# Hybrid encoder block on one core: q in two DRAM tensors, v in SBUF, and an earlier first latent head

## The chip, the core and the metric

One core of a Trainium2 chip runs the whole kernel. The metric is the device time of one execution in microseconds, the median of several runs. The engines are TensorE (PE, with its weight loads as PEld), VectorE (DVE), ScalarE (ACT), GpSimd (POOL) and SyncE (SP), which here only issues DMA transfers. All loads and stores go through SP's one queue, in its order, to 16 DMA engines.

## What is computed

One layer of a bidirectional encoder, 1024 tokens by 1024 features: a SwiGLU block, a mixer, a second SwiGLU block, each between RMS norms and added to the residual. The mixer has one input projection whose columns feed a latent attention (8 heads), a dilated windowed attention (8 heads) and two gates. The part that matters here is the latent attention:

```
q      = (rms_norm(cq) @ w_uq).reshape(S, 8, 64 + 32)      # 64 plain, 32 rotary columns a head
k_nope = (rms_norm(ckv) @ w_uk).reshape(S, 8, 64)
v_a    = (rms_norm(ckv) @ w_uv).reshape(S, 8, 64)
k_a    = concat([k_nope, rope(kr) for every head])
o_a    = softmax(q k_a^T * 96**-0.5) @ v_a                 # dense, 1024 x 1024 a head
```

All products are made to near-float32 accuracy: each operand is split into a high and a low part (`split`, L520: ACT copies the rounded high part, POOL subtracts it), and a product takes three matmuls (`three`, L285).

## The kernel before, in words

**Order of the work.** The stages are Python generators that a planner (`Plan`, L126 to L211) steps through at build time. Each generator yields an engine with a cost (`pe`, `act`, `dve`, `pool`, `dma`, L262 to L278), an `Event` or a `Tokens` count, and the planner serves each engine's queue by rank. The moment at which it calls a step sets where that step is written in the program. The framework's scheduler then fixes the order on each engine; it may put a step ahead of one that was written earlier and whose input or buffer is not there yet. On the chip each engine works strictly in that order.

**Buffers.** SBUF tiles come from three rings: `slot` (21 of 4 KB a partition), `half_slot` (7 of 2 KB) and `big` (14 of 8 KB), L237 to L244. A tile waits until one of its ring is free. In PSUM there are four single banks (`B1`) and two pairs of banks (`S2`).

**Before the stage.** After the first SwiGLU block, the normed input is held, transposed and split, in 8 `big` tiles (`Xm`) until the last column group of the input projection has used it. The column groups ("fillers", `filler_weights` and `chunk_projection`, L1310 and L1421) fill PE while other stages wait. Groups 0 to 3 run before the latent projections, groups 4 to 13 from then on (`HELD`, L113; `m2_done`, L1515).

**The latent projections** (`latent`, from L1656). The compressed q and kv (`cth`, `ctl`: four `big` tiles and two slots) are multiplied by the split weights. For each half of the tokens: `q_rope` (the rotary columns, turned by POOL, transposed, stored), `q_rows(0)`, `k_rows(0)`, four `v_tile`. Then, for head pairs 1 to 3, `q_rows` and `k_rows` of both halves. Each product ends in one PSUM bank; `keep_rows` (L1701) copies it on ACT into a half slot and stores it on SP. Pair i's q of one half is 128 rows by 512 columns in SBUF; in DRAM `qT_d` has 96 rows a head, so the store's target is 2 blocks of 64 rows:

```
rows = qT_d[192 * i : 192 * i + 192, halves[hf]].rearrange("(h e) c -> h e c", e=96)
spawn(keep_rows(ps, qscale, [(rows[:, 0:64, :], 0, P)], [pair_ready[i]]), 4)
```

and the rotary rows of four heads go to 4 blocks of 32 rows (L1753). The rows of k (`kT_d`, L1772) are 128 whole rows that lie together. v goes to `va_d`, 128 whole rows a tile (L1780).

**The heads** (`mla`, L1957; `mla_prep`, L1829). For a head, `mla_prep` loads q (96 rows), then k (64 rows) and the shared rotary k (32 rows), and splits each into two `qkT` slots (ACT, then DVE for q and POOL for k), then loads this head's 64 columns of v from `va_d` (256-byte pieces) and splits them into `vv`. One `nat_tok` lets one of the two loads be prepared at a time. `mla` starts head 0 when `v_written` is set, takes two `proj_tok`, and then starts `mla_prep(0)`; head h+1 is prepared during the second pair of head h. `mla_tile` (L1869) makes one tile of 128 queries: six score matmuls, row maximum on DVE, exponential on ACT (L1892), scaling on POOL (L1902), transposes on PE with casts into a `pt` tile (a `big`; four tokens). `mla_pair` multiplies by `vv`.

Of the kernel before, what the change touches and what calls it, by code (L numbers as in the profile page):

```python
# [9 lines left out]
F32 = mybir.dt.float32  # L10
F32R = mybir.dt.float32r
# [5 lines left out]
S = 1024  # L17
D = 1024
DFF = 2816
P = 128  # L20
NT = S // P
# [104 lines left out]
class Plan:  # L126
# [17 lines left out]
    def spawn(self, gen, rank=5):  # L144
        self.alive.add(gen)
        self._at(self.now, lambda: self._step(gen, rank))
# [73 lines left out]
def _build(tc, es, a, consts, out, dbg):  # L220
# [3 lines left out]
    dr = es.enter_context(tc.tile_pool(name="dr", bufs=1, space=bass.MemoryType.DRAM))  # L224
    V, A, G, T = nc.vector, nc.scalar, nc.gpsimd, nc.tensor
    load = nc.sync.dma_start
    plan = Plan()
    spawn = plan.spawn
# [8 lines left out]
    def slot(shape, dt=F32, name="u"):  # L237
        return sb.tile(shape, dt, tag="u", bufs=NU, name=nm(name))

    def half_slot(shape, dt=F32, name="t"):  # L240
        return sb.tile(shape, dt, tag="t", bufs=NH, name=nm(name))

    def big(shape, dt=F32R, name="g"):
        return sb.tile(shape, dt, tag="g", bufs=NG, name=nm(name))  # L244
# [14 lines left out]
    B1 = Tokens(4)  # L259
# [5 lines left out]
    def act(n, fn):  # L265
        return ("act", 0.04 + n * 0.00088, fn)
# [10 lines left out]
    def dma(kb, fn):  # L277
        return ("dma", kb / 350.0, fn)  # L278
# [19 lines left out]
    kr = keep([P, NT, 32], F32, "kr")  # L298
# [221 lines left out]
    def split(src, hi, lo, n):  # L520
        yield act(n, lambda: A.copy(hi, src))  # L521
        yield pool(n, lambda: G.tensor_sub(lo, src, hi))  # L522
# [609 lines left out]

    h1 = dr.tile([S, D], F32, name="h1")
    h2 = dr.tile([S, D], F32, name="h2")
    qT_d = dr.tile([768, S], F32, name="qT_d")
    kT_d = dr.tile([512, S], F32, name="kT_d")
    kr_d = dr.tile([32, S], F32, name="kr_d")
    va_d = dr.tile([S, 512], F32, name="va_d")
    dqT_d = dr.tile([512, S], F32, name="dqT_d")
    dkT_d = dr.tile([512, S], F32, name="dkT_d")  # L1140
    dv_d = dr.tile([S, 512], F32, name="dv_d")
    lg_d = dr.tile([2 * D, S], F32, name="lg_d")
    ya_d = dr.tile([D, S], F32, name="ya_d")
    oa_d = dr.tile([512, S], F32, name="oa_d")
    ob_d = dr.tile([512, S], F32, name="ob_d")
# [393 lines left out]
    kr_ready, m2_done = Event(NT), Event()  # L1539
    pair_ready, rope_ready, v_ready = [Event(4) for _ in range(4)], Event(6), Event(NT)  # L1540
    v_written = Event()

    def latent():
        yield ffn1_done
# [113 lines left out]
        for c in range(3):  # L1658
            bx = []
# [41 lines left out]
        def keep_rows(ps, scale, stores, evs):  # L1701

            bx = []

            def cp():
                o = half_slot([P, 512], name="o")
                A.mul(o, ps, scale)
                bx.append(o)

            yield act(512, cp)  # L1710
            plan.release(B1)

            def st_():
                for dst, r0, r1 in stores:
                    load(dst, bx[0][r0:r1, :])

            yield dma(256, st_)
            for e in evs:
                plan.set(e)

        def q_rope(hf):

            qr = slot([P, 4, 256], name="qr")
            ready = Event(4)

            def turned(j, ps):
                yield act(256, lambda: A.mul(qr[:, j, :], ps[:, :256], qscale))
                plan.release(B1)
                yield rot_ready
                yield from rope(qr[:, j, :].rearrange("p (h two f) -> p h two f", h=8, two=2), 4 * hf + j, 0, 16)  # L1730
                plan.set(ready)

            for j in range(4):
                ts = slice((4 * hf + j) * P, (4 * hf + j + 1) * P)
                ps = yield from product(256, [
                    (cth[c][:, ts], ctl[c][:, ts], wuq[c][0][:, 512:768], wuq[c][1][:, 512:768]) for c in range(3)
                ])
                spawn(turned(j, ps), 3)

            def rest():  # L1740
                yield ready
                for i in range(2):
                    yield B1
                    bb = []

                    def tr():
                        b = bank()
                        for j in range(4):
                            T.transpose(b[:, j * P : (j + 1) * P], qr[:, j, P * i : P * i + P], ident)
                        bb.append(b)  # L1750

                    yield pe(1024, tr)
                    rows = qT_d[384 * i : 384 * i + 384, halves[hf]].rearrange("(h e) c -> h e c", e=96)  # L1753
                    yield from keep_rows(bb[0], 1.0, [(rows[:, 64:96, :], 0, P)], [rope_ready])

            spawn(rest(), 3)

        def q_rows(i, hf):
            ps = yield from product(512, [
                (wuq[c][0][:, P * i : P * i + P], wuq[c][1][:, P * i : P * i + P], cth[c][:, halves[hf]], ctl[c][:, halves[hf]])  # L1760
                for c in range(3)
            ])
            rows = qT_d[192 * i : 192 * i + 192, halves[hf]].rearrange("(h e) c -> h e c", e=96)
            spawn(keep_rows(ps, qscale, [(rows[:, 0:64, :], 0, P)], [pair_ready[i]]), 4)

        def k_rows(i, hf):
            wh, wl = wkv[0]
# [6 lines left out]
        def v_tile(t):  # L1774
            ts = slice(t * P, (t + 1) * P)
            wh, wl = wkv[1]
            ps = yield from product(512, [
                (cth[3 + c][:, ts], ctl[3 + c][:, ts], wh[:, c, :], wl[:, c, :]) for c in range(2)
            ])
            spawn(keep_rows(ps, 1.0, [(va_d[ts, :], 0, P)], [v_ready]), 3)  # L1780

        def k_rope():
            yield kr_ready
# [45 lines left out]
    def mla_prep(h, hb, ev):  # L1829
        yield pair_ready[h // 2]  # L1830
        yield rope_ready
        for which in range(2):
            yield nat_tok
            bx = Box()

            def ld():
                bx.n = slot([96, S], name="nat")
                if which == 0:
                    load(bx.n, qT_d[96 * h : 96 * h + 96, :])
                else:  # L1840
                    load(bx.n[0:64, :], kT_d[64 * h : 64 * h + 64, :])
                    load(bx.n[64:96, :], kr_d)

            yield dma(512, ld)
            tt = [slot([P, S], F32R, "qkT") for _ in range(2)]
            if which == 0:
                hb.qT = tt
            else:
                hb.kT = tt
            yield act(S, lambda: A.copy(tt[0][:96, :], bx.n))  # L1850
            yield QKSUB[which](S, lambda: (V if QKSUB[which] is dve else G).tensor_sub(tt[1][:96, :], bx.n, tt[0][:96, :]))
            plan.release(nat_tok)

        yield v_ready

        def ldv():
            hb.vn = half_slot([P, NT, 64], name="vn")
            load(hb.vn, va_d[:, 64 * h : 64 * h + 64].rearrange("(t p) c -> p t c", p=P))

        yield dma(400, ldv)  # L1860
        hb.vv = slot([P, NT, P], F32R, "vv")
        yield from split(hb.vn, hb.vv[:, :, 0:64], hb.vv[:, :, 64:128], 512)
        plan.set(ev)

    p_tok = Tokens(3)
# [90 lines left out]

    def mla():  # L1957
        yield v_written
        yield proj_tok
        yield proj_tok  # L1960
        ready = [Event() for _ in range(8)]
        hbs = [Box() for _ in range(8)]
        spawn(mla_prep(0, hbs[0], ready[0]), 3)
        for h in range(8):
            yield ready[h]
            hb = hbs[h]
            hev = Event(4)
            if h == GATES_FROM:
                plan.set(gates_on)
            if h == 7:  # L1970
                plan.set(mla_half)
            for pr in range(4):
                pb = Box()
                pev = [Event(2), Event(2)]
                pb.pt, pb.got = [None, None], [Event(), Event()]

                for qi in range(2):
                    yield p_tok
                    spawn(mla_tile(h, hb, 2 * pr + qi, pb, pev), 2)
                spawn(mla_pair(h, hb, pr, pb, pev, hev), 2)  # L1980
                if pr == 1 and h < 7:
                    spawn(mla_prep(h + 1, hbs[h + 1], ready[h + 1]), 2)

            def fin(ev):
                yield ev
                plan.set(oa_done)
                if oa_done.left == 0:
                    plan.release(pd_tok)

            spawn(fin(hev), 2)  # L1990
# [577 lines left out]
    spawn(second(), 6)  # L2568
    plan.run()
    if dbg is not None:  # L2570
        for nme, src in dict(h1=h1, h2=h2, qT=qT_d, kT=kT_d, kr=kr_d, va=va_d, dqT=dqT_d, dkT=dkT_d, dv=dv_d, lg=lg_d, oa=oa_d, ob=ob_d).items():
            if nme in dbg:
                load(dbg[nme], src)

# [28 lines left out]
```

## Time and profile before

| what | value |
|---|---|
| time, median of 3 runs | 2509.57 us (2507.45 to 2510.3) |
| the profiled execution: its own time | 2505.2 us |
| the profiled execution: span of its instructions | 2503.2 us |
| PE busy | 2311.5 us, 92% of the span |
| mean granted TensorE clock | 0.964 |

The span runs from the first to the last instruction; the 2.0 us between it and the execution's own time lie around it. A line such as "L1850 ACT CAST qkT<-nat [9.72 <-DMA nat<-kr_d]" is read as: the cast of line 1850, which writes qkT from nat, started after its engine had been idle for 9.72 us, and what ended the idle time was the landing of the load of nat from kr_d. SP has no busy time; its rows show how long an issue took. The granted clock has two levels, 1.00 for 2.4 GHz and 0.50 for 1.2 GHz; means lie between.

### The profile page before, as it was taken

The page shows a single profiled execution, that of the slowest core. Times are in us where ns is not written, and L with a number is a line of the kernel's source. Part 1 is how long each engine was busy: PE and PEld are TensorE (multiplying, and loading weights), DVE is VectorE, ACT ScalarE, POOL GpSimd, SP SyncE. Part 2 cuts the span into 40 slices and gives each one's busy share as a digit, 9 for nine tenths or more (in the row PEclk, how much of TensorE's full clock was granted, in tenths as well). Part 3 has the DMA queues.
Part 4 walks back from the last instruction along what each step waited for, and adds up shares of the span by engine and source line. Part 5 has one row for each costly group of instructions (what it writes and reads, how often), then busy time and mean ns, then how long its engine had stood idle before and what let it go on. Part 6 is the DMA issues. An engine that isn't in the chain of part 4 may idle for free. (4 is left out here: it accounts for less than half of the span.)

```text
span 2503.2 us, 30709 instructions
## 1 busy us (share of the span) xinstructions
PE 2311.5 (92%) x11096; PEld 1930.7 (77%) x11096; DVE 1595.3 (64%) x2667; ACT 1042.4 (42%) x1958; POOL 797.8 (32%) x592
## 2 busy tenths in 40 slices
PE   6999999989979995999998889998879999999996
PEld 4888888778769984888887777776668888877885
DVE  8887777655582103666667676347877778773757
ACT  6343343321153334656655555454343334343211
POOL 2000000354483534656543232576300000023545
PEclk8999999999989997999999999899989999999998
DMA  4253443777251233122222222575434434457762
GB/s 152 101 181 126 156 164 130 268 294 259 103 191 45 70 111 96 51 60 73 81 73 84 81 83 70 180 249 197 147 101 168 160 133 170 150 186 286 275 221 101
DMA packets 198007, 364.84 MB, mean 146 GB/s; under 512 B 40608, under 2 KB 112800, under 8 KB 197344
## 3 DMA queue, kind: packets, MB, share of 16 engines
q1 hardware_dynamic: 197856, 362.89, 42.6%
q8 instruction: 87, 1.43, 0.2%
q14 instruction: 64, 0.52, 0.1%
HBM read 240.02 MB, written 122.81 MB: 145 GB/s over the span
## 5 line engine op out<-in xcount | busy, mean ns | idle before, releaser
L675 PE MATMUL s<-xh,wt 128*128 128x512 f32 x1408 | 452.9, 393 | 13.2 <-DVE uu L771 12.2
L522 POOL TENSOR_TENSOR wdb<-rawd,wdb 128x1024 fp32r<-128x1024 f32 x34 | 87.4, 2574 | 958.7 <-ACT wdb L521 958.7
L675 PE MATMUL b<-xh,wt 128*128 128x512 f32 x1056 | 343.4, 392 | 1.9 <-ACT uu L744 0.7
L675 PEld LDWEIGHTS s<-xh,wt 128*128 128x128 f32 x1408 | 266.3, 189 | 72.4 <-issue 13.3
L675 PE MATMUL s<-xl,wt 128*128 128x512 f32 x704 | 275.7, 392 | 0.0
L675 PEld LDWEIGHTS b<-xh,wt 128*128 128x128 f32 x1056 | 199.2, 189 | 44.5 <-DVE wt L649 1.1
L675 PE MATMUL b<-xl,wt 128*128 128x512 f32 x528 | 206.5, 391 | 0.6 <-DVE xl L431 0.6
L1079 PE MATMUL b<-wdb,ha 128*128 128x512 f32 x864 | 203.1, 390 | 3.4 <-POOL wdb L522 3.4
L1079 PE MATMUL s<-wdb,ha 128*128 128x512 f32 x816 | 195.4, 395 | 9.0 <-DVE bacc L1028 4.4
L1079 PEld LDWEIGHTS b<-wdb,ha 128*128 128x128 f32 x864 | 162.3, 188 | 38.0 <-POOL wdb L522 4.3
L1079 PEld LDWEIGHTS s<-wdb,ha 128*128 128x128 f32 x816 | 155.1, 190 | 44.0 <-DVE bacc L1028 5.2
L1442 PE MATMUL b<-xh,wh 128*128 128x512 f32 x384 | 163.4, 425 | 0.0
L1902 POOL TENSOR_TENSOR p<-p,rd 128x1024 f32<-128x1024 f32 x64 | 121.8, 1910 | 104.0 <-DVE rd L1899 102.8
L649 DVE TENSOR_TENSOR wt<-s,wt 128x512 fp32r<-128x512 f32 x176 | 120.1, 710 | 54.1 <-ACT wt L648 54.1
L675 PEld LDWEIGHTS s<-xl,wt 128*128 128x128 f32 x704 | 133.3, 189 | 26.9
L1442 PE MATMUL b<-xl,wh 128*128 128x512 f32 x384 | 153.7, 400 | 0.0
L1442 PE MATMUL b<-xh,wl 128*128 128x512 f32 x384 | 153.6, 400 | 0.0
L522 POOL TENSOR_TENSOR wdb<-td,wdb 128x1024 fp32r<-128x1024 f32 x40 | 107.6, 2694 | 71.4 <-ACT wdb L521 71.4
L426 PE MATMUL b<-cst,p 128*128 128x128 f32 x768 | 107.9, 282 | 23.8 <-DVE ptd L431 14.7
L522 POOL TENSOR_TENSOR wl<-raw,wh 128x512 fp32r<-128x512 f32 (+3 forms) x88 | 108.4, 1250 | 48.7 <-ACT wh L521 42.0
L283 PE MATMUL s<-qkT,qkT 96*128 96x512 f32 x384 | 103.2, 404 | 21.5 <-ACT p L1892 21.5
L426 PEld LDWEIGHTS b<-cst,p 128*128 128x128 f32 x768 | 91.5, 145 | 40.9 <-DVE ptd L431 17.3
(290 smaller groups left out, 5003.2 us busy)
## 6 DMA issues: line engine op xcount, KB each, us to landing
hs_d<-hl SPq DMA_DIRECT2D x140, 512.0 KB
ha<-hs_d SPq DMA_DIRECT2D x70, 1024.0 KB
raw<-in_ffn_w_gate_dram SPq DMA_DIRECT2D x44, 512.0 KB
raw<-in_ffn_w_up_dram SPq DMA_DIRECT2D x44, 512.0 KB
rawd<-in_ffn_w_down_dram SPq DMA_DIRECT2D x44, 512.0 KB
raw<-in_w_in_dram SPq DMA_DIRECT2D x28, 512.0 KB
h<-res SPq DMA_DIRECT2D x16, 512.0 KB
lg_d<-lg SPq DMA_DIRECT2D x32, 256.0 KB
```

The costliest lines, as they stand in the source:

```text
L283: T.matmul(o, l, r, start=(i == 0), stop=(i == n - 1))
L426: T.transpose(b[:rows, i * P : (i + 1) * P], src(i), ident)
L522: yield pool(n, lambda: G.tensor_sub(lo, src, hi))
L649: yield dve(512, lambda: V.tensor_sub(w[:, 1], src, w[:, 0]))
L675: T.matmul(out(), l, r, start=(first and k == 0 and n == 0), stop=(k == 3 and n == 2), skip_group_check=True,)
L1079: T.matmul(ps, l, r, start=(fresh and n == 0), stop=(n == 5), skip_group_check=True)
L1442: T.matmul(bs.ps, l, r, start=(part == 0 and n == 0), stop=(part == 7 and n == 2))
L1902: yield pool(S, lambda: G.tensor_tensor(bx.p, bx.p, bx.rd.broadcast_to([P, S]), op=ALU.mult))
```

## The change

q is kept in DRAM as two tensors, `qn_d` with the 64 plain rows of every head and `qr_d` with the 32 rotary rows, so that each store writes 128 whole rows that lie together; a head's load of q becomes two loads. v is kept in two `big` tiles of SBUF (`va`), from which each head's `vv` is split in two halves; the store to and the loads from `va_d` are gone. Head 0's split q takes a `big` tile in place of two slots, and `mla` starts `mla_prep(0)` before it takes the two `proj_tok`.

```diff
-    qT_d = dr.tile([768, S], F32, name="qT_d")
+    qn_d = dr.tile([512, S], F32, name="qn_d")
+    qr_d = dr.tile([256, S], F32, name="qr_d")
...
-    va_d = dr.tile([S, 512], F32, name="va_d")
...
+    va = [None, None]
...
-                    rows = qT_d[384 * i : 384 * i + 384, halves[hf]].rearrange("(h e) c -> h e c", e=96)
-                    yield from keep_rows(bb[0], 1.0, [(rows[:, 64:96, :], 0, P)], [rope_ready])
+                    yield from keep_rows(bb[0], 1.0, [(qr_d[P * i : P * i + P, halves[hf]], 0, P)], [rope_ready])
...
-            rows = qT_d[192 * i : 192 * i + 192, halves[hf]].rearrange("(h e) c -> h e c", e=96)
-            spawn(keep_rows(ps, qscale, [(rows[:, 0:64, :], 0, P)], [pair_ready[i]]), 4)
+            spawn(keep_rows(ps, qscale, [(qn_d[P * i : P * i + P, halves[hf]], 0, P)], [pair_ready[i]]), 4)
...
-            spawn(keep_rows(ps, 1.0, [(va_d[ts, :], 0, P)], [v_ready]), 3)
+            spawn(keep_v(ps, t), 3)
+
+        def keep_v(ps, t):
+            def cp():
+                if t % 4 == 0:
+                    va[t // 4] = big([P, 4, 512], F32, name="va")
+                A.copy(va[t // 4][:, t % 4, :], ps)
+
+            yield act(512, cp)
+            plan.release(B1)
+            plan.set(v_ready)
...
-                    load(bx.n, qT_d[96 * h : 96 * h + 96, :])
+                    load(bx.n[0:64, :], qn_d[64 * h : 64 * h + 64, :])
+                    load(bx.n[64:96, :], qr_d[32 * h : 32 * h + 32, :])
...
-            tt = [slot([P, S], F32R, "qkT") for _ in range(2)]
+            if h == 0 and which == 0:
+                hl = big([P, 2, S], name="qk0")
+                tt = [hl[:, 0, :], hl[:, 1, :]]
+            else:
+                tt = [slot([P, S], F32R, "qkT") for _ in range(2)]
...
-        def ldv():
-            hb.vn = half_slot([P, NT, 64], name="vn")
-            load(hb.vn, va_d[:, 64 * h : 64 * h + 64].rearrange("(t p) c -> p t c", p=P))
-
-        yield dma(400, ldv)
         hb.vv = slot([P, NT, P], F32R, "vv")
-        yield from split(hb.vn, hb.vv[:, :, 0:64], hb.vv[:, :, 64:128], 512)
+        for kb in range(2):
+            ks = slice(4 * kb, 4 * kb + 4)
+            yield from split(va[kb][:, :, 64 * h : 64 * h + 64], hb.vv[:, ks, 0:64], hb.vv[:, ks, 64:128], 256)
...
         yield v_written
-        yield proj_tok
-        yield proj_tok
         ready = [Event() for _ in range(8)]
         hbs = [Box() for _ in range(8)]
         spawn(mla_prep(0, hbs[0], ready[0]), 3)
+        yield proj_tok
+        yield proj_tok
```

## Rows read from the trace of the kernel before

**Rows 1.** The page, part 1: busy time, share of the span, instructions.

```profile
PE 2311.5 (92%) x11096; PEld 1930.7 (77%) x11096; DVE 1595.3 (64%) x2667; ACT 1042.4 (42%) x1958; POOL 797.8 (32%) x592
```

**Rows 2.** Stretches: length, busy of PE PEld DVE ACT POOL, clock, DMA share, GB/s.

```profile
935.00:945.00 10.00, 2.92 (x13) 2.11 (x13) 0.00 (x0) 1.79 (x3) 0.67 (x1) 0.90 0.21 78
...
955.00:965.00 10.00, 0.00 (x0) 0.00 (x0) 0.00 (x0) 0.00 (x0) 0.00 (x0) 0.50 0.28 90
965.00:975.00 10.00, 1.94 (x5) 1.55 (x6) 0.33 (x2) 5.60 (x12) 4.48 (x5) 0.50 0.52 149
```

**Rows 3.** Waits of PE, 860 to 1000: total us, times, longest.

```profile
PE s L283 <- ACT p L1892: 21.5, 1, 21.5
PE b L283 <- ACT o L1707: 8.6, 2, 7.1
```

**Rows 4.** Waits of ACT, 880 to 985: total us, times, longest.

```profile
ACT o L1707 <- DMA qT_d<-o: 6.7, 3, 2.9
```

**Rows 5.** Timeline of SP's queue: start, time of the issue, transfer.

```profile
932.69 1.16 SPq L1842 DMA_DIRECT2D nat<-kr_d  x1
...
934.92 4.90 SPq L1715 DMA_DIRECT2D kT_d<-o  x1
...
955.17 4.77 SPq L1858 DMA_DIRECT2D vn<-va_d  x1
```

**Rows 6.** Single microseconds as stretches; the last two columns are the DMA's.

```profile
937.00:938.00 1.00, 0.72 (x4) 0.26 (x2) 0.00 (x0) 0.00 (x0) 0.00 (x0) 1.00 0.13 49
940.00:941.00 1.00, 0.00 (x0) 0.00 (x0) 0.00 (x0) 0.00 (x0) 0.00 (x0) 1.00 0.69 260
...
964.00:965.00 1.00, 0.00 (x0) 0.00 (x0) 0.00 (x0) 0.00 (x0) 0.00 (x0) 0.50 0.13 49
```

**Rows 7.** Timeline of PE: start, length, line, form, count, idle before.

```profile
928.54 0.74 PE L283 MATMUL b<-ct,wuh 128*128 128x512 f32 x2 [1.54 <-ACT o L1707]
...
937.33 0.39 PE L283 MATMUL b<-cth,wul 128*128 128x512 f32 x1
944.80 1.22 PE L283 MATMUL b<-ct,wuh 128*128 128x512 f32 x2 [7.08 <-ACT o L1707]
...
947.52 4.01 PE L283 MATMUL s<-qkT,qkT 96*128 96x512 f32 x12
973.06 2.93 PE L283 MATMUL s<-qkT,qkT 96*128 96x512 f32 x6 [21.52 <-ACT p L1892]
...
983.95 0.48 PE L1442 MATMUL b<-xh,wh 128*128 128x512 f32 x1
```

**Rows 8.** Timeline of ACT: the casts of head 0 and the first exponential.

```profile
926.95 1.04 ACT L1850 CAST qkT<-nat 96x1024 fp32r<-96x1024 f32 x1 [6.08 <-DMA nat<-qT_d]
...
943.21 1.04 ACT L1850 CAST qkT<-nat 96x1024 fp32r<-96x1024 f32 x1 [9.72 <-DMA nat<-kr_d]
...
969.17 0.62 ACT L521 CAST vv<-vn 128x512 fp32r<-128x512 f32 x1 [20.27 <-DMA vn<-va_d]
...
970.51 1.28 ACT L1892 ACT_TABLE_LOAD   x1
971.80 1.11 ACT L1892 ACTIVATE p<-s,negm 128x1024 f32<-128x1024 f32 x1
```

**Rows 9.** Timeline of DVE: head 0's first row maximum.

```profile
950.18 1.23 DVE L1886 TENSOR_REDUCE negm<-s 128x1 f32<-128x1024 f32 x1 [20.93 <-PE s L283]
```

**Rows 10.** The tile qkT: q's subtraction, ns min/median/max, first and last start.

```profile
L1851 DVE TENSOR_TENSOR qkT<-nat,qkT x8: 1202/2024/3316, 928.0 to 1218.1; 96x1024 fp32r<-96x1024 f32 x8
```

**Rows 11.** The tile vn: v's subtraction on POOL, ns min/median/max.

```profile
L522 POOL TENSOR_TENSOR vv<-vn,vv x8: 1262/1292/1297, 969.9 to 1232.7; 128x512 fp32r<-128x512 f32 x8
```

**Rows 12.** Stretches: the first stall, the heads, the stage behind them.

```profile
926.80:928.60 1.80, 0.26 (x2) 0.06 (x1) 0.57 (x1) 1.65 (x3) 0.00 (x0) 1.00 0.83 212
...
985.00:1300.00 315.00, 310.09 (x1833) 268.55 (x1831) 208.71 (x352) 201.25 (x385) 182.36 (x109) 0.99 0.24 68
1300.00:1600.00 300.00, 265.62 (x1335) 223.40 (x1336) 203.43 (x583) 154.36 (x384) 86.63 (x52) 0.93 0.28 81
```

More of the change, by code (lines that the diff above doesn't have):

```diff
@@ L2570, in _build @@
     if dbg is not None:
-        for nme, src in dict(h1=h1, h2=h2, qT=qT_d, kT=kT_d, kr=kr_d, va=va_d, dqT=dqT_d, dkT=dkT_d, dv=dv_d, lg=lg_d, oa=oa_d, ob=ob_d).items():
+        for nme, src in dict(h1=h1, h2=h2, kT=kT_d, kr=kr_d, dqT=dqT_d, dkT=dkT_d, dv=dv_d, lg=lg_d, oa=oa_d, ob=ob_d).items():
             if nme in dbg:
```

## The prediction

> **What bounds the kernel now.** I read the page first. PE is busy 92% of the span [rows 1], so a change that doesn't touch PE's own work can win only where PE stands still or runs at its lower clock. Then the stretches around the lines that the diff touches. In the ten microseconds from 935, from 955 and from 965 PE works 2.92, 0.00 and 1.94 us, the granted clock falls to 0.50, and no other engine is full either: ACT and POOL have 0.00 from 955 to 965 [rows 2]. This stage is bound by waits.
>
> The waits name them. PE waited 21.5 us for the first exponential and 8.6 us for copies out of PSUM [rows 3]: 30.1 us. Behind both stands ACT, which works in order: it stood 6.7 us for half slots whose q had not yet been stored [rows 4], 9.72 us before the cast of head 0's k, for the rotary k's load, and 20.27 us before the cast of head 0's v, for v's load [rows 8]. The exponential is written behind that cast and began at 971.80 [rows 8]; its input was there long before, since the row maximum began at 950.18 and took 1.23 [rows 9].
>
> So what is late is the DMA. The rotary k's load was issued at 932.69 [rows 5] and let ACT go on at 943.21 [rows 8], 10.5 us for 128 KB; v's load, issued at 955.17 [rows 5], let it go on at 969.17 [rows 8], 14 us. Yet the 16 DMA engines are not full. In single microseconds the share is 0.13 and the rate 49 GB/s, again and again, and 0.69 and 260 GB/s in another [rows 6]. 0.13 of 16 is two engines. What is left in those microseconds is q's stores, the only transfers in this stage whose target is 2 blocks; a k store of the same 256 KB is 128 rows in one block. At 49 GB/s a q store takes 256 KB / 49 = 5.3 us (an estimate), six of them from pair 1 to 3 take 32 us on the same two engines, and every later load has a share on those two and queues behind them. The issues of 4.90 and 4.77 us on SP [rows 5] say the same: the queue was full.
>
> **The change, part by part.**
>
> *q as whole rows.* It removes the blocks: each q store becomes a store of k's kind, about 1 us at 260 GB/s [rows 6] in place of 5.3. The backlog then does not form, half slots come free, and PE's 8.6 us [rows 3] go. Each head loads q in two transfers: 8 more issues, about 1.16 us each by the worst such row [rows 5], on a queue that is no longer blocked; the heads' stage has PE at 310 of 315 us [rows 12] and hides them. The first of these loads waits on SP for the rotary q stores and holds the stores of pair 1 behind it, as today; seven half slots cover that. Should they not, PE stalls as in the 1.54 us row [rows 7].
>
> *v in SBUF.* Eight stores and eight loads go. ACT's copy is the same work. The wait of 20.3 us before v's cast goes: its input is now made by ACT itself, before. Splitting in two halves costs POOL at most a second 1.29 us a head [rows 11], 10 us over 315 in which POOL is busy 182 [rows 12]: hidden. For head 0 they lie on an idle POOL.
>
> *The earlier start.* Worth nothing, I think. q's cast of head 0 already ran at 926.95 [rows 8], before the last products, so the two tokens were not what it waited for.
>
> *Head 0's q in a `big` tile.* This is a new wait. `Xm` holds 8 of the 14, the compressed q and kv 4, `va` 2: the ring is full, and the 15th tile is free only when the last `q_rows` has read its input. So q's cast moves from 926.95 to the end of that product. If it stood on ACT ahead of copies that free banks for that same product, the program would never end, so the scheduler must put it behind them; then only the last two copies stand behind it.
>
> *The sum, in the clock of the profiled execution.* The last product's first matmul ran at 944.80 after stalls of 1.54 and 7.08 us [rows 7]; without them at 944.80 - 8.62 = 936.2. That is when q's buffer comes free. The pace between is (937.33 - 928.54) / 38 = 0.231 us a matmul [rows 7], so six end at 937.6. q's cast takes 1.04 [rows 8], to 937.2. Its subtraction takes 1.20 alone and up to 3.32 when POOL works beside it; I take the median, 2.02 [rows 10], to 939.3. The first two of six score matmuls don't need it, the other four end 4 x 0.231 later, at 940.2. The maximum takes 1.23 [rows 9] and some 0.3 of hand-over: the exponential begins at 941.8, not 971.80 [rows 8]. That is 30.0 us. The table load of 1.28 [rows 8] falls into ACT's wait for the maximum; were it not hidden, 28.7. With the subtraction at its ends, 28.7 to 30.8.
>
> From the exponential to the first filler lie 983.95 - 971.80 = 12.15 us [rows 7, 8]; the order there stays. Its first six score matmuls took 2.93 us at the lower clock [rows 7] against 6 x 0.231 = 1.4 at the full one, but POOL's scaling runs beside them; I take 1 of the 1.5. Sum: 31 us. The bound from above: PE cannot get back more than its 30.1 us of waits plus the lower clock, which is (947.52 + 4.01 - 944.80) - 18 x 0.231 = 2.6 and 1.5, and some transposes: about 35.
>
> *A rule weighed.* After the stall of 1.54 us the clock stayed at 1.00 [rows 12], so I count head 0 at the full level; it fell only in the long waits [rows 2]. The Trainium skill (TensorE: Matmul & The Clock Gate, "A second HAM failure mode: psum-queue depth-cycling") tells of a kernel in which short idle moments between groups of matmuls kept the clock going back and forth between its levels. By the row the sum stays 31; by that rule it would be the rival on the clock below.
>
> So the profiled execution would take 2505.2 - 31 = 2474.2. The median of the runs stands 4.4 above the profiled execution (2509.57 to 2505.2), so the forecast is **2478.5**.
>
> **The rivals.**
>
> *Only v's wait goes.* If the two busy DMA engines are not q's stores, the 8.6 us stay, and so do the score matmuls at 947.52. The maximum ends at 950.18 + 1.23, the exponential starts at 951.7: a gain of 20, so 2489.5. For it: the long wait names v's load alone. Against: rates of 49 GB/s beside 260 [rows 6].
>
> *The ring of 14.* While head 0 lasts, `Xm` 8, `va` 2 and its q 1 leave 3 tiles for `pt` where there were 4 tokens. If its four pairs then ran one behind the other, each would take the 12.15 us above, 48.6 in all, against 315 / 8 = 39.4 for a head now [rows 12]: 9.2 us given back, 2487.7. Against: the fillers need no `pt`, and PE can take them.
>
> *The clock.* If small gaps hold the clock down as in the stage behind the heads, 0.93 against 0.99 [rows 12], for all heads: 315 x 0.06 = 19 us given back, 2497.5. Against: PE's gaps there are 34 us in 300, in the heads 5 in 315.
>
> *Slower: the fillers run out.* The planner's times shift with the shorter preparation of each head, and the order of fillers among heads with them. If they are spent early, late heads run as the stage behind does: 34.4 / 300 idle and 0.06 of clock, about 17 us lost in 100 [rows 12]. It decides from 31 / 0.17 = 180 us on, that is 4.6 of the 8 heads; all heads would lose 54 and give 2509.6 - 31 + 54 = 2533. Against: groups are held back by tokens and by the fifth head (`GATES_FROM`), not by time.
>
> *It doesn't do what it says.* The planner places head 0's loads as before and the new full ring costs what the loads gave: no change, about 2509.
>
> **How the numbers follow.** The forecast, a gain of 26 to 36, has 0.75; only v's wait 0.08; the ring 0.07; the clock 0.03; no change 0.03; slower 0.04. A measurement of this kernel can tell about 0.2%, 5 us, from no change. The forecast and the first three rivals all lie beyond that: faster 0.93, same 0.03, slower 0.04. The range takes the bound of 35 us and some 3 us by which a changed order elsewhere can move the time, 2471, and reaches to the first rival, 2490; that leaves out the clock, no change and slower, and the tails of the order.
>
> **What would show it.** Right: after, no stretch of the stage at 0.13 and 49 GB/s; issues of k's stores near 1 us or less; PE's waits for L1707 gone; q's cast of head 0 at about 936, later than now; the first exponential between 940 and 943; the clock at 1.00 throughout the stage; PE's idle time in the 315 us of heads still under 10. Wrong: an exponential near 952 (only v's wait), a clock of 0.9 in the heads, PE waiting for casts to `pt` in head 0, or idle time in the later heads. Only the stage's 31 us should differ; if the stage gives them and the time doesn't follow, the later order took them.

## The result, and the profile after

The changed kernel takes 2475.69 us (median of 4 runs, 2472.70 to 2477.72), the kernel before 2509.94 (median of 4, 2507.45 to 2510.34): 34.25 us less, a ratio of 0.9868 with a 95% interval of 0.9852 to 0.9883. The profiled executions took 2505.2 before and 2472.7 after, their spans 2503.2 and 2470.5 us. The forecast was 2478.5, with 2474.2 for the profiled execution.

The page of the kernel after, part 1, to be read against [rows 1]:

```profile
PE 2310.1 (94%) x11096; PEld 1928.9 (78%) x11096; DVE 1602.3 (65%) x2667; ACT 1042.7 (42%) x1966; POOL 798.0 (32%) x600
```

PE's busy time is 1.4 us less than before, the span 32.7 us less; the gain is idle time. The stage's stretches in the kernel after:

```profile
core 0: us, PE busy (x) PEld busy (x) DVE busy (x) ACT busy (x) POOL busy (x), PEclk, DMA share, GB/s
925.00:935.00 10.00, 10.00 (x46) 8.29 (x45) 0.80 (x1) 4.53 (x7) 0.00 (x0) 1.00 0.67 251
935.00:945.00 10.00, 7.36 (x39) 5.49 (x38) 5.79 (x9) 7.77 (x17) 5.04 (x5) 1.00 0.43 131
945.00:955.00 10.00, 9.42 (x59) 7.63 (x57) 8.54 (x12) 8.11 (x15) 6.80 (x7) 1.00 0.03 8
955.00:965.00 10.00, 10.00 (x60) 8.78 (x60) 6.68 (x11) 6.75 (x14) 10.00 (x8) 1.00 0.22 60
...
985.00:1300.00 315.00, 310.78 (x1820) 267.80 (x1818) 207.21 (x395) 200.33 (x407) 174.08 (x110) 1.00 0.24 66
```

Where PE had 2.92 us of the ten from 935 and none of those from 955 [rows 2], it has 7.36 and 10.00, and the granted clock is 1.00 throughout. What PE waited for from 860 to 1000, after, all of it:

```profile
PE b L426 <- POOL p L1913: 2.0, 3, 0.9
PE s L283 <- ACT p L1903: 1.2, 1, 1.2
PE b L1442 <- DVE pt L431: 0.5, 1, 0.5
```

The 21.5 and 8.6 us of [rows 3] are down to 1.2 and nothing. The last stores of the stage on SP, after, and the next load of q (start, time of the issue):

```profile
933.10 0.32 SPq L1716 DMA_DIRECT2D kT_d<-o  x1
935.14 0.32 SPq L1716 DMA_DIRECT2D qn_d<-o  x1
936.50 0.32 SPq L1716 DMA_DIRECT2D kT_d<-o  x1
936.91 0.45 SPq L1848 DMA_DIRECT2D nat<-qn_d  x1
```

None of these issues is held; before, those behind q's stores took 4.90 and 4.77 us [rows 5]. Of the single microseconds from 890 to 990, nine had the share of 0.13 at 49 GB/s before; after, none has. Head 0's preparation and first exponential on ACT, after:

```profile
922.77 0.70 ACT L521 CAST vv<-va 128x256 fp32r<-128x256 f32 x2
...
933.11 1.05 ACT L1864 CAST qk<-nat 96x1024 fp32r<-96x1024 f32 x1
...
936.50 1.28 ACT L1903 ACT_TABLE_LOAD   x1
938.48 1.11 ACT L1903 ACTIVATE p<-s,negm 128x1024 f32<-128x1024 f32 x1 [0.70 <-DVE negm L1897]
```

v's cast, which waited 20.27 us for a load and ended 2 us ahead of the exponential, with the table load between them [rows 8], is now two casts that are done 15 us ahead of it, and the table load lies in ACT's wait for the row maximum. The first exponential moved from 971.80 [rows 8] to 938.48. On DVE and PE, in the same microseconds after:

```profile
934.20 1.22 DVE L1865 TENSOR_TENSOR qk<-nat,qk 96x1024 fp32r<-96x1024 f32 x1 [56.26 <-ACT qk L1864]
937.22 2.58 DVE L1897 TENSOR_REDUCE negm<-s 128x1 f32<-128x1024 f32 x2 [1.80 <-PE s L283]
```

```profile
932.68 0.39 PE L283 MATMUL b<-ct,wul 128*128 128x512 f32 x1
...
934.27 0.61 PE L283 MATMUL b<-ct,wuh 128*128 128x512 f32 x2
...
935.40 0.39 PE L283 MATMUL b<-ct,wul 128*128 128x512 f32 x1
935.63 2.91 PE L283 MATMUL s<-qkT,qk 96*128 96x512 f32 x12
939.73 1.65 PE L283 MATMUL s<-qkT,qk 96*128 96x512 f32 x6 [1.19 <-ACT p L1903]
```

PE goes from the last latent product (934.27 to 935.63) into head 0's scores with no gap.

**How far a mark can be trusted.** The code ahead of the stage is the same in both kernels, yet it does not end at the same time. The first transposes of the input projection's `rn` on PE, in the kernel before and in the kernel after:

```profile
843.01 0.60 PE L1413 MATMUL b<-cst,rn 128*128 128x128 f32 x4
```

```profile
841.61 0.60 PE L1413 MATMUL b<-cst,rn 128*128 128x128 f32 x4
```

So 1.4 us of the 33.3 at the exponential came from before the stage, and 31.9 from it. This offset was between 1.4 us early and 3.9 us late in the executions profiled here. "Net" below means a shift of an instruction against the kernel before with the offset of its own execution taken out.

### The profile page after: what moved, and what is told of

It is laid out like the page before. It is cut to its first block, busy times and chain, and to the rows that moved or that the text cites. A ratio compares the mean times of both kernels' runs of the same rounds, so it can differ in the third digit from the quotient of the medians.

```text
span 2470.5 us, 30753 instructions
## 1 busy us (share of the span) xinstructions
PE 2310.1 (94%) x11096; PEld 1928.9 (78%) x11096; DVE 1602.3 (65%) x2667; ACT 1042.7 (42%) x1966; POOL 798.0 (32%) x600
## 5 line engine op out<-in xcount | busy, mean ns | idle before, releaser
L648 ACT CAST wt<-s 128x512 fp32r<-128x512 f32 x176 | 103.2, 621 | 34.1 <-DVE s L619 16.8
```

The costliest lines, as they stand in the source:

```text
L648: yield act(512, lambda: A.copy(w[:, 0], src))
```

## The experiments

The runs of the kernel before that stand beside the first four gave a median of 2508.42 (7 runs), beside the last two 2509.77 (7 runs). Each kernel's profile is one execution. Theory: q's stores with targets of 2 blocks run on two DMA engines, and what is queued behind them is late. Rivals: the layout or the traffic is at fault and not the count of blocks; or only v's trip through DRAM costs time.

**q as whole rows, alone** (v stays in DRAM, head 0's q in slots, the start where it was):

```diff
-    qT_d = dr.tile([768, S], F32, name="qT_d")
+    qn_d = dr.tile([512, S], F32, name="qn_d")
+    qr_d = dr.tile([256, S], F32, name="qr_d")
```

> The kernel before with only q as two tensors of whole rows; v still goes through DRAM and head 0's q sits in slots. Theory (q's stores in two blocks run on 2 of the 16 DMA engines, and everything behind them is late): no microsecond of the stage at share 0.13 and 49 GB/s, PE's 8.6 us of waits for copies gone, and v's load, now without a backlog, lands within some 3 us of its issue, so the first exponential runs between 938 and 946 instead of 971.8 and the time is 2476 to 2485. Rival (v's load itself is what was slow): the 8.6 us go, a wait of over 10 us before v's cast stays, the first exponential at 955 or later, time 2494 to 2502.

Measured: 2477.38 us, a ratio of 0.9874 (0.9856 to 0.9892): 31.0 of the 34.25 us. The first exponential came 28.7 us earlier, net, and no single microsecond from 890 to 990 has the share of 0.13 at 49 GB/s. In its PE waits, its ACT waits, and its stretch from 945:

```profile
PE s L283 <- ACT p L1892: 4.4, 1, 4.4
```

```profile
ACT vv L521 <- DMA vn<-va_d: 2.6, 1, 2.6
```

```profile
945.00:955.00 10.00, 8.28 (x34) 7.00 (x35) 4.50 (x9) 7.63 (x16) 8.11 (x9) 0.66 0.20 47
```

v still goes through DRAM, and its cast now waits 2.6 us for it, not 20.3: v's load was late because of q's stores. The rest costs PE one wait of 4.4 us and some time at the lower clock.

**v in SBUF, alone** (q stays one tensor with 96 rows a head):

```diff
-            spawn(keep_rows(ps, 1.0, [(va_d[ts, :], 0, P)], [v_ready]), 3)
+            spawn(keep_v(ps, t), 3)
```

> The kernel before with only v kept in SBUF; q is stored in blocks as before. Theory: q's stores keep two DMA engines busy, so the stretches at 0.13 and 49 GB/s stay, the load of the rotary k stays about 10 us late and PE's waits of about 8 us for copies stay; only v's wait of 20.3 us goes, the first exponential runs at about 951.7, time 2487 to 2492. Rival (v's load was the whole loss): the time of the full change, 2473 to 2479, with the first exponential near 938.

Measured: 2494.03 us, 0.9935 (0.9920 to 0.9950), a gain of 14.4, some 2 us short of the expected times. The first exponential came 20.4 us earlier, net. Its PE waits, one microsecond of it, and the exponential on ACT:

```profile
PE b L283 <- ACT o L1707: 9.4, 1, 9.4
PE s L283 <- ACT p L1899: 3.9, 2, 2.8
```

```profile
939.00:940.00 1.00, 0.00 (x0) 0.00 (x0) 0.00 (x0) 0.00 (x0) 0.00 (x0) 1.00 0.13 49
```

```profile
954.93 1.11 ACT L1899 ACTIVATE p<-s,negm 128x1024 f32<-128x1024 f32 x1 [0.70 <-DVE negm L1893]
```

The two busy DMA engines are there, PE's wait for copies is there, and only v's wait is gone: my first rival as it was drawn, to the microsecond at the exponential (954.93 less this execution's offset of 3.5 is 951.4; the rival had 951.7). It lost more after that: raw weights for the fillers stand in the same queue, ACT waited 6.6 us for them ahead of the third exponential, and there the net shift is 15.5 us in place of 20.4.

The two parts gain 31.0 and 14.4 alone and 34.25 together: they remove largely the same wait.

**Head 0's q in two slots**, all else as after:

```diff
-            if h == 0 and which == 0:
-                hl = big([P, 2, S], name="qk0")
-                tt = [hl[:, 0, :], hl[:, 1, :]]
-            else:
-                tt = [slot([P, S], F32R, "qkT") for _ in range(2)]
+            tt = [slot([P, S], F32R, "qkT") for _ in range(2)]
```

> The changed kernel with head 0's q in two slots instead of a tile of the ring of 14. Theory: the new wait for a tile of that ring costs nothing, since the cast finishes before the last product: q's cast runs some 10 us earlier (near 920 instead of 933), the first exponential stays at 938 to 940 and the time within 3 us of the changed kernel, 2473 to 2479. Rival (slots are short, and the tile of the other ring is what lets head 0 be ready): the first exponential at 945 or later and 2482 or more. Third (the tile costs pt buffers in head 0): 3 to 9 us faster, 2467 to 2473.

Measured: 2478.77 us, 0.9873 (0.9854 to 0.9892), not to be told from the change. In the clock of the execution after, q's cast ran at 919.4, as expected. The first exponential came 31.9 us earlier, net (after: 31.9), the ninth 32.7 (after: 33.4). The `big` tile is neither a cost nor a gain here, and there was no shortage of tiles for `pt`. The stretch from 945 and the PE waits that go with it:

```profile
945.00:955.00 10.00, 9.31 (x44) 7.50 (x45) 5.64 (x11) 7.22 (x17) 8.64 (x9) 0.83 0.16 40
```

```profile
PE s L283 <- ACT p L1899: 1.2, 1, 1.2
PE b L426 <- POOL p L1909: 1.2, 2, 0.6
```

**Each head's block a transfer of its own**: q again in one tensor of 96 rows a head, with the old room between the blocks, but two stores of one block instead of one of two (four instead of one for the rotary rows); loads as before:

```diff
-            ... [(qn_d[P * i : P * i + P, halves[hf]], 0, P)] ...
+            ... [(qT_d[96 * (2 * i + u) : 96 * (2 * i + u) + 64, halves[hf]], 64 * u, 64 * u + 64) for u in range(2)] ...
```

> The changed kernel, but q again in one DRAM tensor with 96 rows a head, so that the rows of a store do not lie together; each head's block of 64 (or 32) rows is a transfer of its own in place of one transfer of 2 (or 4) blocks. Theory (the number of blocks in a transfer sets how many DMA engines it uses): no stretch at 0.13 and 49 GB/s, first exponential before 945, time 2472 to 2482. Rival (rows that do not lie together are slow to write, however they are cut): stretches at 49 GB/s or less stay, PE waits for copies out of PSUM again, time 2485 to 2495.

Measured: 2476.86 us, 0.9869 (0.9850 to 0.9889). The layout was the old one, no single microsecond from 890 to 990 has the share of 0.13 at 49 GB/s, PE does not wait for copies out of PSUM, and the time is that of the change. The room between the blocks costs nothing; two tensors are not needed. The first exponential came 28.1 us earlier, net (at 945.97, which is 943.7 in the clock of the execution before; I had expected it before 945), less than after: PE waited 1.7 us for the low part of a k from POOL, and the clock fell behind that (last section).

**q interleaved**: the converse. The target of a store is the same 128 dense rows as after, but written as 2 blocks, each of every second row:

```diff
-            spawn(keep_rows(ps, qscale, [(qn_d[P * i : P * i + P, halves[hf]], 0, P)], [pair_ready[i]]), 4)
+            rows = qn_d[P * i : P * i + P, halves[hf]].rearrange("(e h) c -> h e c", h=2)
+            spawn(keep_rows(ps, qscale, [(rows, 0, P)], [pair_ready[i]]), 4)
...
-                    load(bx.n[0:64, :], qn_d[64 * h : 64 * h + 64, :])
+                    load(bx.n[0:64, :], qn_d[P * (h // 2) : P * (h // 2) + P, :].rearrange("(e two) c -> two e c", two=2)[h % 2])
```

> The changed kernel, but the plain rows of q of a head pair stand interleaved in the same dense 128 rows of DRAM (row 2e + h), so a store's target is again 2 blocks, of every second row, with no room between the rows of a store. Theory (the count of blocks in one transfer sets how many DMA engines carry it): stretches of single microseconds at a share of 0.13 and 49 GB/s come back for q's stores, PE waits again for the copies to half slots (4 to 10 us in all), and the time is about that of v in SBUF alone, 2487 to 2497 us. Rival (it is the room between the blocks in the old tensor, or rows that don't lie together): no such stretches, and 2473 to 2480 us.

Measured: 2488.47 us, 0.9912 (0.9895 to 0.9928), 12.8 us above the change. Its PE waits, one microsecond, three issues on SP, and two casts and copies on ACT:

```profile
PE s L283 <- ACT p L1904: 10.9, 2, 6.7
PE b L283 <- ACT o L1708: 0.9, 1, 0.9
```

```profile
948.00:949.00 1.00, 0.00 (x0) 0.00 (x0) 0.00 (x0) 0.13 (x1) 0.00 (x0) 0.50 0.13 49
```

```profile
941.06 4.80 SPq L1716 DMA_DIRECT2D kT_d<-o  x1
945.95 0.49 SPq L1716 DMA_DIRECT2D qn_d<-o  x1
946.54 5.56 SPq L1716 DMA_DIRECT2D kT_d<-o  x1
```

```profile
948.87 0.60 ACT L1708 ACTIVATE o<-b 128x512 f32<-128x512 f32 x1 [5.71 <-DMA qn_d<-o]
...
968.35 1.04 ACT L1865 CAST qkT<-nat 96x1024 fp32r<-96x1024 f32 x1 [6.00 <-DMA nat<-qr_d]
```

The share of 0.13 and the 49 GB/s are back, with the same bytes to the same 128 rows, in another order. It is k's store, itself one block, whose issue is held for 4.80 and 5.56 us, about the 5.3 us that a q store takes at 49 GB/s. The loss comes in two places. ACT, which needs a half slot back, waited 5.71 us for a q store before it could go on to the first exponential, and PE waited 6.67 us for that. Then, inside head 0, ACT waited 6.00 us for the load of head 1's rotary q, whose issue (958.37) came behind the held ones; the exponentials written behind that cast were late, and PE waited another 4.22 us. The net shift against the kernel before is 24.9 us at the first exponential, 25.4 at the fourth and 18.9 at the fifth, behind that cast. One detail was not as expected: PE's wait stands against the exponential and not, as I had written, against the copies (0.9 us); the copies and the cast hold up ACT, and an exponential is what is behind them there.

**k in 2 blocks**: q as after, but k in a tensor of 96 rows a head:

```diff
-            spawn(keep_rows(ps, 1.0, [(kT_d[P * i : P * i + P, halves[hf]], 0, P)], [pair_ready[i]]), 6)
+            rows = kT_d[192 * i : 192 * i + 192, halves[hf]].rearrange("(h e) c -> h e c", e=96)
+            spawn(keep_rows(ps, 1.0, [(rows[:, 0:64, :], 0, P)], [pair_ready[i]]), 6)
```

> The changed kernel, but k is stored into a tensor with 96 rows a head, so that each store of k has a target of 2 blocks of 64 rows, as q's had before. Theory (the blocks, whoever stores them): k's stores now run on two engines at about 49 GB/s, some 5.3 us each, the loads of head 0 land late, PE stands 4 to 10 us for copies, and the time is 2487 to 2497 us. Rival (only q's stores matter, because they lead the queue, or q's layout): 2473 to 2480 us.

Measured: 2494.43 us, 0.9934 (0.9916 to 0.9952), 18.7 us above the change. Its PE waits, a copy before the first exponential and a cast behind the fourth on ACT, and one microsecond:

```profile
PE s L283 <- ACT p L1904: 13.5, 2, 7.9
```

```profile
944.01 0.60 ACT L1708 ACTIVATE o<-b 128x512 f32<-128x512 f32 x1 [4.84 <-DMA kT_d<-o]
...
969.73 1.04 ACT L1865 CAST qkT<-nat 96x1024 fp32r<-96x1024 f32 x1 [9.64 <-DMA nat<-qr_d]
```

```profile
953.00:954.00 1.00, 1.00 (x6) 0.82 (x5) 0.75 (x2) 0.73 (x2) 1.00 (x3) 0.50 0.13 49
```

With the blocks given to k instead of q, the slow stores and the held copies move with them. So it is the shape of one transfer, whoever makes it. Here too PE's wait stands against the exponential (13.5 us) and only 1.0 us against the copies, and the larger part is the second place: 5.59 us for the first exponential, 7.87 us inside head 0, behind ACT's wait of 9.64 us for head 1's rotary q. The net shift is 26.3 us at the first exponential and 15.9 at the fifth. The loads that I had expected to be late were head 0's; the one that cost most was head 1's, behind the same queue. The Trainium skill (DMA: Bandwidth & Descriptors, "Why a DMA increments its semaphore by 16 and not by 1") says that the number of engines is the largest, up to 16, that divides the slowest dimension of both sides; the 0.13 of 16 engines for 2 blocks, here and in [rows 6], agrees. The profile gives the mean share of the 16 engines and not which of them work: that there are two is read off the share.

**The earlier start of head 0** was not run: with the two tokens taken before or after the start, in the kernel before and in the changed one, the program has the same instructions in the same order on all five engines. That edit is worth nothing, as the prediction had it.

## Why the prediction was right, point by point

- *What bounds the stage: q's stores on two engines.* Right, and now shown from both sides: the count of blocks alone brings the rate of 49 GB/s and the late work back (q interleaved, k in 2 blocks), and taking it away alone, in the old layout, gives the time of the change.
- *q as whole rows: the 8.6 us go.* Right. The added issue costs no more than the bound of 1.16 that I took: the load of q's plain rows took SP 0.45 us (the last of SP's rows above).
- *v in SBUF: the wait of 20.3 goes.* It goes, but the prediction gave the gain to the wrong part. With q whole the wait is 2.6 us with v still in DRAM, and the time 2477.38 against 2475.69, which the intervals don't separate. The second halves of the split on POOL cost nothing to be seen: PE has 310.78 of the 315 us from 985, against 310.09 [rows 12].
- *Head 0's q in a `big` tile is a new wait.* There is a wait, shorter than I made it. The cast began at 933.11; in the clock of the execution before that is 934.5, not 936.2. The buffer was free before the end of the last q product (934.27): the cast came right behind a copy on ACT that ended at 933.08, and the product's first input chunk had been read by then, a third into it (the row at 932.68 ends at 933.07). Which of the two it waited for is not shown. The slots in its place gave the same first exponential, so nothing hung on it.
- *The subtraction, taken at 2.02 us.* Mis-sized: it took 1.22, with POOL idle beside it, close to the 1.20 that is its least [rows 10] (which is not its time alone in every case, as I had it: the one at 1105.50, before, took 1.20 us with POOL's scaling beside it from 1105.66). It ended at 935.42, before PE was done with the last latent product at 935.63. So it was not on the path: that ran from the last product over six score matmuls (to 937.22) and a maximum to 938.48. In the clock of the execution before that is 939.9, where I had 941.8, and just ahead of the 940 to 943 that I had named as a sign; 1.9 us more than the 30.0.
- *From the exponential to the first filler, 12.15 us, "the order there stays".* It did not stay. After, the first filler's matmul starts at 957.92, 19.4 us behind the exponential, because PE now does more of head 0 first (scores, transposes and products, 9.42 of the ten us from 945). PE was not idle there, so this cost nothing; the ninth exponential is 33.4 us earlier, net. The 1 us that I allowed for the clock in head 0 fits these 1.5 (33.4 less 31.9).
- *"Only the stage's 31 us should differ."* Not quite: some 4.6 us more came in head 2 (the net shift is 33.2 us at its first exponential and 37.8 at that of head 3). There PE, before, waited 3.00 us for a copy out of PSUM, and the mean clock of the ten us from 1070 was 0.83, against 1.00 after. PE and DVE of the kernel before:

```profile
1075.75 0.74 PE L426 MATMUL b<-cst,p 128*128 128x128 f32 x4 [3.00 <-DVE o L1952]
```

```profile
1071.21 2.81 DVE L1493 TENSOR_TENSOR pj<-pj,tb 64x512 f32<-64x512 f32 x1 [2.40 <-ACT pj L1487]
...
1075.19 0.42 DVE L1952 TENSOR_TENSOR o<-b,o 64x256 f32<-64x256 f32 x1
```

DVE stood behind the rotation of a projected column group and a maximum. That wait is gone in every kernel here that keeps v in SBUF (with v alone the net shift grows from 14.9 to 19.4 us there) and still 2.7 us with q alone; the largest PE wait of that stretch after is 0.8. Why v in SBUF shifts these steps against each other was not traced. The gain then shrinks from 35.6 us net at the last exponential to 31.3 at the end, over 1200 us of unchanged code; at the end q alone has as much (31.2). I could not put this return to a cause. Over the same stretch the kernel with q in slots gave back 8.8 us and that with head blocks apart gained 3.2; so single executions don't settle it, and it is not shown to be a cost of the change.
- *The sum.* 31 us from 2505.2; the profiled executions give 32.5, 1.4 of which is the offset. The medians give 34.25, and the difference lies in the runs' spread of 5 us. That the time came within 2.8 us of the forecast is in part luck: what came in head 2 (4.6 us) and what was given back behind the heads (4.3) stand in no term of the sum, and they nearly cancel.
- *The rivals.* "Only v's wait goes" is what v alone does, not the change. The ring of 14 cost nothing (slots for `big`). The clock stayed at 1.00 in the heads, where it was 0.99 [rows 12]. The fillers did not run out: PE has 267.05 of the 300 us from 1300 in the kernel after, 265.62 before [rows 12]. The kernel does what it says.

## What to carry to other kernels

Look at DMA rates in single microseconds: a steady 49 GB/s at a share of 0.13 between bursts of 250 is a transfer on few engines, and its victim is whatever comes behind it in the queue, here v's load, a k store and head 1's load of q, whose own shape was not the cause. Ask of each DMA what the slowest dimension of either side is, and if it is 2, write it as two transfers, or turn the layout so that the rows are whole. Before giving a wait's whole length to the transfer named in it, take away what is queued ahead of it: that was worth 31 us of 34 here, and the removal of the waited-for transfer 14, most of them the same.

## What the hardware showed that I had not expected

- *Four blocks, four engines.* Other stores of the same program, of dilated q and k, go to targets of 4 blocks. They show a share of 0.26, a quarter of the engines, at 102 GB/s, in the kernel after, with PE busy beside them; they cost nothing there:

```profile
869.00:870.00 1.00, 1.00 (x7) 0.81 (x5) 0.00 (x0) 0.03 (x1) 0.00 (x0) 1.00 0.26 102
```

- *The clock falls after waits that look alike.* After, PE waited 1.19 us for the first exponential and twice up to 0.93 us soon behind it, and the granted clock stayed at 1.00; before, it stayed there after 1.54 us: PE's timeline has that wait, and the clock was 1.00 nine us behind it [rows 7, 6] (the stretch that the prediction read for this [rows 12] ends with the wait and doesn't show it). With head blocks apart it fell to 0.50 behind a wait of 1.70 us (PE's timeline, then stretches of that kernel):

```profile
939.75 0.73 PE L283 MATMUL s<-qkT,qk 96*128 96x512 f32 x2 [0.31 <-ACT qkT L1862]
942.18 4.63 PE L283 MATMUL s<-qkT,qk 96*128 96x512 f32 x10 [1.70 <-POOL qkT L1863]
```

```profile
942.00:943.00 1.00, 0.82 (x2) 0.73 (x3) 0.00 (x0) 0.09 (x1) 1.00 (x3) 0.54 0.65 156
...
945.00:946.00 1.00, 1.00 (x4) 0.81 (x3) 0.94 (x1) 0.03 (x1) 0.00 (x0) 0.50 1.11 407
```

Ten score matmuls then took 4.63 us, where twelve took 2.91 after. With head 0's q in slots, waits of 1.2 and 0.6 us were followed by a mean clock of 0.83 in the ten from 945 (its row stands above). What separates these cases was not settled.
- *Unchanged code varies by some 5 us.* The offset of the `rn` transposes, from 1.4 us early to 3.9 us late, arises ahead of everything that any of these kernels changes. A difference of a few us between two single executions is not yet a difference between two kernels.
